# Transposing finished feed-forward blocks by DMA in 16-bit halves instead of on TensorE

## The chip, the cores and the metric

The kernel runs on one core of one Trainium2 chip. The metric is the device time of one execution, in microseconds, as the median over runs. One core has five engines with an instruction stream each: TensorE (PE in the profile; its weight loads are shown as PEld), VectorE (DVE), ScalarE (ACT), GpSimd (POOL) and SyncE (SP, which here only issues DMAs). Each takes its own instructions in order and waits on semaphores for the others.

## What is computed

A decoder trunk of two layers on 512 tokens of width 1024. Each layer is a half-step SwiGLU feed-forward block, a token mixing part (three kinds of attention, gated and merged), and a second half-step SwiGLU, with RMS norms around each. In the kernel the four feed-forward blocks are named a0, c0, a1, c1. What matters here is the SwiGLU:

```
def _swiglu(t, w_gate, w_up, w_down):
    return (jax.nn.silu(t @ w_gate) * (t @ w_up)) @ w_down
...
    for l in range(DEPTH):
        f = _swiglu(_rmsnorm(h, ffn1_pre_g[l]), ffn1_w_gate[l], ffn1_w_up[l], ffn1_w_down[l])
        h = h + 0.5 * _rmsnorm(f, ffn1_post_g[l])
...
        f = _swiglu(_rmsnorm(h, ffn2_pre_g[l]), ffn2_w_gate[l], ffn2_w_up[l], ffn2_w_down[l])
        h = h + 0.5 * _rmsnorm(f, ffn2_post_g[l])
```

The hidden width is 2816, 22 tiles of 128 columns. All data is float32; each factor of a product is split into a high and a low part, and three matmuls stand for one product.

## The kernel before

**A feed-forward block** (`ffn`). Sixteen of the 22 hidden tiles are computed in two column groups (`ci` 0 and 1) of 1024 columns. In each group the gate and then the up projection is one 2x2 block matrix product (tokens in two halves, output columns in two halves) done by seven block products instead of eight (`token_product`, products 0 to 6 in the order 0, 2, 1, 3, 4, 5, 6). So the main stretch of a block is: gate group 0 (G0), up group 0 (U0), gate group 1 (G1), up group 1 (U1), then the down projection's fourteen block products (`product`), with six remaining hidden tiles computed plainly in between. A product runs over four tiles `kk` of the contraction, and for each over two output banks `e`, with three matmuls of 128x512 each (lines 204 to 206 of the profile): 24 matmuls. `PLAN` writes the order out by hand; a queue object feeds it, loads weights ahead, and a scheduler then fixes each engine's order.

**Weights** arrive by DMA from SyncE's queue (lines 248 and 296) into raw tiles, are combined where a product needs a difference (line 326, VectorE; tiles `tg`, `tu`, `bt`), cast to the high part by ScalarE (line 181, `wh`) and subtracted by VectorE to the low part (line 182, `wl`). `wh` and `wl` have four buffers each, which are two products' worth.

**What a product leaves.** Its sums lie in two PSUM banks, with tokens on the partitions. Products 2 and 3 are copied out by ScalarE (line 775), products 4 and 5 are added by VectorE (line 777), and in an up group the products 1 and 6 are multiplied from PSUM with the gate's block (line 779), those of 4 and 5 after the addition (line 784). So after the products 1, 4, 5 and 6 of an up group one block of the hidden activations is finished, 128 partitions x 1024 (four hidden tiles' quarter for two token tiles), in the gate's tile (`sa`, `sc`). Products 3, 5 and 6 add on in the banks that product 0 opened.

**The transposes.** The down projection needs the hidden activations with hidden columns on the partitions (`hr`, from which `first_factor` makes its operands). So every finished block is transposed. `turn` does it in the next product, after that product's third tile `kk`: eight TensorE transposes of 128x128 (line 800), four into each of two PSUM banks, and a copy of each bank into `hr` by ScalarE (line 802). Over the kernel that is 4 feed-forward blocks x 2 up groups x 4 blocks = 32 times.

Of the kernel before, what the change touches and what calls it, by code (L numbers as in the profile page):

```python
# [9 lines left out]
F32 = mybir.dt.float32  # L10
F32R = mybir.dt.float32r
BF16 = mybir.dt.bfloat16
AF = mybir.ActivationFunctionType
ALU = mybir.AluOpType
AX = mybir.AxisListType
# [2 lines left out]
P = 128  # L18
# [4 lines left out]
def kernel(  # L23
# [38 lines left out]
    nc = tc.nc  # L62
    _, S, D = x.shape
# [3 lines left out]
    ND = D // P  # L67
# [21 lines left out]
    make_identity(nc, ident)  # L89
    ident16 = cst.tile([P, P], BF16, name="ident16")  # L90
    eps_t = cst.tile([P, 1], F32, name="eps_t")
    nc.vector.memset(eps_t[:], D * EPS)
    one_t = cst.tile([P, 1], F32, name="one_t")
    nc.vector.memset(one_t[:], 1.0)
    causal16 = cst.tile([P, P], BF16, name="causal16")
    sel = cst.tile([104, NH], F32, name="sel")

    def tmp(name):
        return sb.tile([P, S], F32, tag="f32t", bufs=5, name=name)
# [3 lines left out]
    def stile(shape, tag, name, dt=F32R):  # L103
        return sb.tile(shape, dt, tag=tag, bufs=BUFS[tag], name=name)
# [4 lines left out]
    def pbank(tag, name):  # L109
        return ps.tile([P, S], F32, tag=tag, bufs=4, name=name)  # L110
# [67 lines left out]
    def split(h_ap, l_ap, src, scale=None, later=False):  # L178
# [4 lines left out]
        else:  # L183
            both = [nc.scalar.activation(h_ap, src, AF.Copy, scale=scale)]  # L184
            make = lambda: nc.vector.scalar_tensor_tensor(l_ap, src, scale, h_ap.bitcast(F32), ALU.mult, ALU.subtract)  # L185
# [7 lines left out]
    def sigmoid_neg(t, z, c):  # L193

        b, minus = nbgate[:, c[0], c[1]:c[1] + 1], bgate[:, c[0], c[1]:c[1] + 1]
        nc.scalar.activation(t, z, AF.Abs, bias=b)
        nc.scalar.activation(t, t, AF.Exp, scale=-1.0)
        nc.scalar.activation(t, t, AF.Ln, bias=one_t[:])  # L198
        nc.vector.scalar_tensor_tensor(t, z, minus, t, ALU.max, ALU.add)  # L199
        nc.scalar.activation(t, t, AF.Exp, scale=-1.0, bias=minus)  # L200

    def mm3(pt, lh, ll, rh, rl, start, stop, free=False):

        nc.tensor.matmul(pt, lh, rh, start=start, stop=False, skip_group_check=free)  # L204
        nc.tensor.matmul(pt, lh, rl, start=False, stop=False, skip_group_check=free)  # L205
        nc.tensor.matmul(pt, ll, rh, start=False, stop=stop, skip_group_check=free)  # L206
# [271 lines left out]
    def rstd(st, a, b=None):  # L478

        s, m, y, w = st[:, a:a + 1], st[:, 3:4], st[:, 4:5], st[:, 5:6]  # L480
        if b is None:
            nc.scalar.activation(y, s, AF.Ln, bias=eps_t[:])
            nc.vector.tensor_scalar(m, s, D * EPS, None, ALU.add)
# [113 lines left out]
    ORDER = (0, 2, 1, 3, 4, 5, 6)  # L597
    SUM = (0, 1, 2, 0, 2, 0, 0)
    TO = ((0, 0), (0, 0), (1, 1), (0, 1), (0, 1), (1, 1), (1, 0))
    park = [nc.dram_tensor(f"park{i}", (NT, P, D), F32, kind="Internal").ap() for i in range(2 * L)]  # L600

    def ffn(l, src, wg, wu, wd, dst, name, spare, parked, plan, aside=None):
# [4 lines left out]


        hid, st = {}, {}
        hr = {}  # L610
        f0 = NC * FC
        tags = ["q"] * 2 + ["o"] * 4
        act = lambda k, c=FULL: quad_act(src.us)(k, c)
# [1 line left out]
        def hidden_rows(i):  # L615
            if i not in hr:
                hr[i] = stile([P, FC // 2, S], ("k", "tri")[i // 2], f"hr{name}_{i}", F32)
            return hr[i]
# [114 lines left out]
        def in_product(n):  # L733
            if n in (0, 1, 6):
                i, j = ((0, 0), (0, 1), None, None, None, None, (1, 1))[n]
                return [block(i, j, part) for part in range(2)]
            return st["u", n]

        def token_product(ci, up, n, uns):

            nm = f"{name}{'gu'[up]}_{ci}_{n}"
            if n in (0, 1, 2):
                st["c", n] = [pbank("z" if n == 0 else "mm", f"pw{nm}_{e}") for e in range(2)]
            if n == 1:
                for e in range(2):
                    nc.scalar.copy(st["c", 1][e][:], st["c", 0][e][:])
            if n == 0:
                if not up:
                    st["s", ci] = {}
            pts = st["c", SUM[n]]  # L750
            h, l = in_product(n)
            opens, ends = n in (0, 2), n in (1, 4, 6)
            for un in uns:
                for k in range(un.nk):
                    kk = un.k0 + k
                    for e in range(2):
                        c = slice(e * P, (e + 1) * P)
                        mm3(pts[e][:], h[:, kk, c], l[:, kk, c], un.h[:, k], un.l[:, k], opens and kk == 0,
                            ends and kk == ND // 2 - 1, free=True)
                        yield 3 * S * PE_US  # L760
                    if kk == ND // 2 - 2:
                        yield from turn("z")
            if n == 0:
                return
            q = TO[n]
            g = st["s", ci]
            if not up and q not in g:
                g[q] = stile([P, FC // 2, S // 2], "f", f"s{name}_{ci}_{q[0]}{q[1]}", F32)[:]
            g = g[q]
            r = hidden_rows(2 * ci + q[1])[:, :, HALVES[q[0]]] if up else g  # L770
            for e in range(2):
                p = pts[e][:].rearrange("p (f q) -> p f q", f=2)
                re, ge = r[:, 2 * e:2 * e + 2], g[:, 2 * e:2 * e + 2]
                if n in (2, 3):
                    nc.scalar.copy(re, p)
                elif n in (4, 5):
                    nc.vector.tensor_tensor(re, re, p, ALU.add)
                elif up:
                    nc.vector.tensor_tensor(ge, p, ge, ALU.mult)
                else:  # L780
                    nc.scalar.activation(re, p, AF.Silu)
            if n in (4, 5):
                if up:
                    nc.vector.tensor_tensor(g, r, g, ALU.mult)
                else:
                    nc.scalar.activation(r, r, AF.Silu)
            if up and n in (1, 4, 5, 6):
                st["turn"] = (f"{nm}", g, r)

        def turn(tag):  # L790

            nm, g, r = st.pop("turn", (None, None, None))
            if nm is None:
                return
            g = g.rearrange("p f q -> p (f q)")
            for b in range(2):
                pt = pbank(tag, f"ht{nm}_{b}")
                for f in range(2):
                    for e in range(2):
                        nc.tensor.transpose(pt[:, (2 * f + e) * P:(2 * f + e + 1) * P],  # L800
                                            g[:, e * S + (2 * b + f) * P:][:, :P], ident[:])
                nc.scalar.copy(r[:, 2 * b:2 * b + 2], pt[:].rearrange("p (f q) -> p f q", f=2))
                yield 0.4
# [42 lines left out]
        def product(at, uns):  # L846
            ci, n = DOWN[at]
            first, last = ci == 0, ci == NC - 1
            if at == 0:
                RINGS["o"] = 2  # L850
                dst.begin()
            if at + 1 < len(DOWN):
                first_factor(*DOWN[at + 1])
            if first and n in (0, 2):
                st["b", SUM[n]] = [pbank("z", f"pd{name}_{n}_{e}") for e in range(2)]
            pts = st["b", SUM[n]]
            h, l = st.pop(("a", ci, n))
            opens, ends = first and n in (0, 2), last and n in (1, 4, 6)
            for un in uns:
                for k in range(un.nk):  # L860
                    kk = un.k0 + k
                    for e in range(2):
                        c = slice(e * P, (e + 1) * P)
                        mm3(pts[e][:], h[:, kk, c], l[:, kk, c], un.h[:, k], un.l[:, k], opens and kk == 0,
                            ends and kk == FC // 2 - 1, free=True)
                        yield 3 * S * PE_US
                    if kk == FC // 2 - 2:
                        yield from turn("mm")
            if not last:
                return  # L870
            if n == 0:
                st["b", 1] = [pbank("z", f"pd{name}_1_{e}") for e in range(2)]
                for e in range(2):
                    nc.scalar.copy(st["b", 1][e][:], pts[e][:])
                return
            i, hf = TO[n]
            for e in range(2):
                f = dst.fs[2 * i + e][:, HF[hf]]
                if n in (4, 5):
                    nc.vector.tensor_tensor(f, f, pts[e][:], ALU.add)  # L880
                else:
                    nc.scalar.copy(f, pts[e][:])
# [767 lines left out]

    wps, wsb = pbank("z", "warm"), tmp("warm").bitcast(BF16)
    nc.vector.memset(wsb[:, 0:S], 0.0)
    mc = None
    for l in LAYERS:
        i, mn = 3 * l, []
# [44 lines left out]
```

## Time and profile before

| | |
|---|---|
| median of 3 runs | 2388.64 us (2386.66 to 2390.05) |
| profiled execution, its own time | 2394.11 us |
| its span in the profile | 2392.4 us |
| mean granted TensorE clock | 0.998 |
| TensorE busy | 2371.8 us, 99% of the span |
| VectorE busy | 1807.0 us, 76% |
| ScalarE busy | 1416.7 us, 59% |
| DMA, mean over the span | 141 GB/s |

Busy times are merged spans, so matmuls that overlap count once. A row of a group gives line, engine, operation, the tiles written and read with buffer numbers left out, the count, the merged busy time and the mean of one instruction in ns, and the idle time of the engine before it with what ended it. A row of the timeline gives the start, the length, engine, line and operation; several equal ones may be merged (x8). In the waits and the chain, "PE pwc0u L206" names engine, tile and line. `pwc0u` is the PSUM tile of the up products of the block c in layer 0.

### The profile page before, as it was taken

The page shows a single profiled execution, that of the slowest core. Times are in us where ns is not written, and L with a number is a line of the kernel's source. Part 1 is how long each engine was busy: PE and PEld are TensorE (multiplying, and loading weights), DVE is VectorE, ACT ScalarE, POOL GpSimd, SP SyncE. Part 2 cuts the span into 40 slices and gives each one's busy share as a digit, 9 for nine tenths or more (in the row PEclk, how much of TensorE's full clock was granted, in tenths as well). Part 3 has the DMA queues.
Part 4 walks back from the last instruction along what each step waited for, and adds up shares of the span by engine and source line. Part 5 has one row for each costly group of instructions (what it writes and reads, how often), then busy time and mean ns, then how long its engine had stood idle before and what let it go on. Part 6 is the DMA issues. An engine that isn't in the chain of part 4 may idle for free.

```text
span 2392.4 us, 31521 instructions
## 1 busy us (share of the span) xinstructions
PE 2371.8 (99%) x11975; PEld 2007.0 (84%) x11975; DVE 1807.0 (76%) x2358; ACT 1416.7 (59%) x2242; POOL 75.1 (3%) x134
## 2 busy tenths in 40 slices
PE   9999999999999999999999999999999999999998
PEld 7788889888888888888888888889888888888887
DVE  8876877676777689778788778766767767887685
ACT  6655565576766555554655545656777664655544
POOL 1000000000111000000000000000001100000000
PEclk9999999999999999999999999999999999999999
DMA  6654455223323655544645544542323235555443
GB/s 203 185 149 142 159 189 146 80 82 87 89 72 106 197 173 176 146 144 152 222 139 166 167 150 144 200 123 71 94 75 97 80 115 194 164 180 159 150 150 141
DMA packets 232172, 338.22 MB, mean 141 GB/s; under 512 B 10683, under 2 KB 125395, under 8 KB 232021
## 3 DMA queue, kind: packets, MB, share of 16 engines
q1 hardware_dynamic: 231924, 336.18, 44.9%
q8 instruction: 94, 1.54, 0.3%
q14 instruction: 58, 0.47, 0.1%
q0 software_dynamic: 96, 0.03, 0.0%
HBM read 319.39 MB, written 16.78 MB: 141 GB/s over the span
## 4 chain that ended last, share of the span: by engine, by line
PE 90%; DVE 4%; DMA 2%; ACT 2%; issue 1%; SPq 0%; POOL 0%; DVEq 0%; ACTq 0%
PE pg L204 3%; PE pg L206 3%; PE pg L205 3%; PE pdc L205 3%; PE pdc L206 3%; PE pda L205 3%; PE pdc L204 3%; PE pda L204 3%; PE pda L206 3%; PE pb L206 2%; PE pb L204 2%; PE pb L205 2%; PE pq L204 1%; PE pq L205 1%; PE pk L205 1%
## 5 line engine op out<-in xcount | busy, mean ns | idle before, releaser
L204 PE MATMUL pg<-us_a,wh_wg 128*128 128x512 f32 x384 | 151.2, 394 | 0.0
L206 PE MATMUL pg<-us_a,wl_wg 128*128 128x512 f32 x384 | 149.9, 390 | 0.0
L205 PE MATMUL pg<-us_a,wh_wg 128*128 128x512 f32 x384 | 149.8, 390 | 0.0
L205 PE MATMUL pda<-wl_da,aha 128*128 128x512 f32 x224 | 87.9, 392 | 0.2 <-DVE wl_da L182 0.2
L205 PE MATMUL pdc<-wl_dc,ahc 128*128 128x512 f32 x224 | 87.7, 392 | 0.0
L181 ACT CAST wh_da<-raw_da 128x1024 fp32r<-128x1024 f32 x50 | 52.2, 1051 | 59.9 <-PE pda L206 18.7
L206 PE MATMUL pda<-wh_da,ala 128*128 128x512 f32 x224 | 87.4, 390 | 0.0
L206 PE MATMUL pdc<-wh_dc,alc 128*128 128x512 f32 x224 | 87.3, 390 | 0.0
L204 PE MATMUL pda<-wh_da,aha 128*128 128x512 f32 x224 | 86.8, 390 | 0.0
L204 PE MATMUL pdc<-wh_dc,ahc 128*128 128x512 f32 x224 | 86.8, 390 | 0.0
L206 PEld LDWEIGHTS pg<-us_a,wl_wg 128*128 128x128 f32 x384 | 72.1, 188 | 15.3
L182 DVE TENSOR_TENSOR wl_da<-raw_da,wh_da 128x1024 fp32r<-128x1024 f32 x50 | 60.8, 1223 | 31.4 <-ACT wh_da L181 31.0
L204 PEld LDWEIGHTS pg<-us_a,wh_wg 128*128 128x128 f32 x384 | 72.2, 188 | 14.0
L205 PEld LDWEIGHTS pg<-us_a,wh_wg 128*128 128x128 f32 x384 | 72.2, 188 | 14.0
L182 DVE TENSOR_TENSOR wl_dc<-raw_dc,wh_dc 128x1024 fp32r<-128x1024 f32 x50 | 61.0, 1223 | 30.2 <-ACT wh_dc L181 29.8
L181 ACT CAST wh_dc<-raw_dc 128x1024 fp32r<-128x1024 f32 x50 | 52.4, 1051 | 51.6 <-PE pdc L206 19.0
L185 DVE SCALAR_TENSOR_TENSOR wl_wg<-raw_wg,wh_wg 128x1024 fp32r<-128x1024 f32 x48 | 58.4, 1221 | 21.6 <-ACT wh_wg L184 21.6
L199 DVE SCALAR_TENSOR_TENSOR ga<-pg,bgate,ga 128x512 f32<-128x512 f32 x48 | 35.9, 747 | 49.6 <-ACT ga L198 49.6
L181 ACT CAST wh_uc<-raw_uc 128x1024 fp32r<-128x1024 f32 x44 | 46.3, 1052 | 43.8 <-PE pwc1u L206 10.3
L181 ACT CAST wh_ua<-raw_ua 128x1024 fp32r<-128x1024 f32 x44 | 46.1, 1051 | 32.6 <-PE pwa1u L206 10.3
L184 ACT ACTIVATE wh_wg<-raw_wg 128x1024 fp32r<-128x1024 f32 x48 | 50.5, 1057 | 24.1 <-PE pv L1092 11.7
L182 DVE TENSOR_TENSOR wl_uc<-raw_uc,wh_uc 128x1024 fp32r<-128x1024 f32 x44 | 53.7, 1220 | 12.1 <-ACT wh_uc L181 12.1
(651 smaller groups left out, 8006.3 us busy)
## 6 DMA issues: line engine op xcount, KB each, us to landing
raw_da<-in_ffn_w_down_dram SPq DMA_DIRECT2D x66, 512.0 KB, 4.4
raw_dc<-in_ffn_w_down_dram SPq DMA_DIRECT2D x66, 512.0 KB, 3.9
raw_ga<-in_ffn_w_gate_dram SPq DMA_DIRECT2D x52, 512.0 KB, 3.8
raw_ua<-in_ffn_w_up_dram SPq DMA_DIRECT2D x52, 512.0 KB, 4.1
raw_gc<-in_ffn_w_gate_dram SPq DMA_DIRECT2D x52, 512.0 KB, 3.8
raw_uc<-in_ffn_w_up_dram SPq DMA_DIRECT2D x52, 512.0 KB, 3.8
raw_wg<-in_w_gate_dram SPq DMA_DIRECT2D x48, 512.0 KB, 3.5
raw_wo<-in_w_out_dram SPq DMA_DIRECT2D x24, 512.0 KB, 3.6
```

The lines of the kernel that those rows point to most:

```text
L181: both = [nc.scalar.copy(h_ap, src)]
L182: make = lambda: nc.vector.tensor_tensor(l_ap, src, h_ap.bitcast(F32), ALU.subtract)
L184: both = [nc.scalar.activation(h_ap, src, AF.Copy, scale=scale)]
L185: make = lambda: nc.vector.scalar_tensor_tensor(l_ap, src, scale, h_ap.bitcast(F32), ALU.mult, ALU.subtract)
L199: nc.vector.scalar_tensor_tensor(t, z, minus, t, ALU.max, ALU.add)
L204: nc.tensor.matmul(pt, lh, rh, start=start, stop=False, skip_group_check=free)
L205: nc.tensor.matmul(pt, lh, rl, start=False, stop=False, skip_group_check=free)
L206: nc.tensor.matmul(pt, ll, rh, start=False, stop=stop, skip_group_check=free)
```

## The change

The blocks of products 1, 4 and 6 of every up group are transposed by DMA, the block of product 5 by TensorE as before. In the second tile `kk` of the product behind, ScalarE splits the float32 words of the block into two tiles of 16-bit words (low and high halves, `th`). In the third tile, SyncE issues for each of them one transposing DMA, SBUF to SBUF, 128x1024 16-bit words (`tr`). Three products further on, ScalarE puts the transposed words back into `hr`, every second 16-bit word, the low half in the first tile and the high half in the third. The products of the down projection call the same step, so the last blocks of a group finish there. The tiles for it come from the five temporary buffers (`tmp`) and, for products 1 and 6, from the buffer tagged "rs". The scheduler may set each of these instructions earlier or later on its engine; in the changed program's order the put-backs stand earlier than the source has them, a few instructions behind the splits.

```
+    DMA_TURNS, OWN_PLANES = {1: 0, 4: 0, 6: 0}, (1, 6)
...
-        hr = {}
+        hr, turns = {}, []
...
                         yield 3 * S * PE_US
+                    dma_turn(kk)
                     if kk == ND // 2 - 2:
                         yield from turn("z")
...
-            if up and n in (1, 4, 5, 6):
+            if up and n in DMA_TURNS:
+                turns.append([nm, g, (2 * ci + q[1], q[0]), n in OWN_PLANES, -DMA_TURNS[n], None, None])
+            elif up and n in (1, 4, 5, 6):
                 st["turn"] = (f"{nm}", g, r)
+
+        def dma_turn(kk):
+
+            for one in turns:
+                nm, g, (row, i), own, age, parts, planes = one
+                if kk == 1 and age == 0:
+                    one[5] = parts = [tmp(f"th{nm}_{h}")[:].bitcast(U16) for h in range(2)]
+                    words = g.rearrange("p f q -> p (f q)").bitcast(U16)
+                    for h in range(2):
+                        nc.scalar.copy(parts[h], words[:, h::2])
+                if kk == 2 and age == 0:
+                    one[6] = planes = ([stile([P, 2, 2 * S], "rs", "tr" + nm, U16)[:, h] for h in range(2)] if own else
+                                       [tmp(f"tr{nm}_{h}")[:].bitcast(U16) for h in range(2)])
+                    for h in range(2):
+                        nc.sync.dma_start_transpose(planes[h].rearrange("p (r q) -> p r q", q=P), parts[h])
+                if kk in (0, 2) and age == 3:
+                    r, h = hidden_rows(row)[:].bitcast(U16), kk // 2
+                    nc.scalar.copy(r[:, :, i * S + h:(i + 1) * S:2].rearrange("p f (e q) -> p e f q", e=2),
+                                   planes[h].rearrange("p (e f q) -> p e f q", e=2, q=P))
+                if kk == ND // 2 - 1:
+                    one[4] += 1
+            turns[:] = [one for one in turns if one[4] < 4]
...
                         yield 3 * S * PE_US
+                    dma_turn(kk)
                     if kk == FC // 2 - 2:
                         yield from turn("mm")
```

More of the change, by code (lines that the diff above doesn't have):

```diff
@@ L12 @@
 BF16 = mybir.dt.bfloat16
+U16 = mybir.dt.uint16
 AF = mybir.ActivationFunctionType
```

## The prediction

> **What bounds the kernel now.** The page comes first, for the busy shares and for the chain that ended last.
>
> ```profile
> span 2392.4 us, 31521 instructions
> PE 2371.8 (99%) x11975; PEld 2007.0 (84%) x11975; DVE 1807.0 (76%) x2358; ACT 1416.7 (59%) x2242; POOL 75.1 (3%) x134
> PE 90%; DVE 4%; DMA 2%; ACT 2%; issue 1%; SPq 0%; POOL 0%; DVEq 0%; ACTq 0%
> ```
>
> TensorE is busy 99% of the span and carries 90% of the chain, so time taken from TensorE's stream comes off the end unless another engine then holds TensorE up. The profiled execution took 2394.11 us around its span of 2392.4; the median of the runs is 2388.64, which is 5.47 less. I work out a difference against the profiled execution and take the same difference from the median. A measurement of this kernel can tell about 0.2%, or 4.8 us, from no change.
>
> Next I read what an up group's stretch looks like, since the whole change lies there and in the products just behind. The windows are the two up groups of one layer's second feed-forward block (DVE is VectorE, ACT is ScalarE).
>
> ```profile
> core 0: us, PE busy (x) PEld busy (x) DVE busy (x) ACT busy (x) POOL busy (x), PEclk, DMA share, GB/s
> 922.00:961.00 39.00, 38.80 (x180) 32.03 (x179) 32.22 (x30) 21.08 (x26) 0.00 (x0) 1.00 0.59 175
> 1002.60:1041.50 38.90, 38.71 (x180) 31.86 (x179) 32.42 (x32) 23.64 (x29) 0.00 (x0) 1.00 0.46 136
> ```
>
> TensorE is full here too, VectorE has some 6.6 us free in 39, ScalarE 15 to 18, and the DMA engines are about half busy, at the full granted clock (1.00).
>
> **Part 1, what is removed: TensorE's transposes.** All rows of the line that transposes finished blocks, by feed-forward block, and one row of its copy out of PSUM:
>
> ```profile
> L800 PE MATMUL hta0u<-ident,sa x64: 270/273/303, 98.4 to 205.1; 128*128 128x128 f32 x64
> L800 PE MATMUL htc0u<-ident,sc x64: 271/273/273, 942.5 to 1048.6; 128*128 128x128 f32 x64
> L800 PE MATMUL hta1u<-ident,sa x64: 270/273/273, 1285.0 to 1392.3; 128*128 128x128 f32 x64
> L800 PE MATMUL htc1u<-ident,sc x64: 270/273/273, 2130.1 to 2236.1; 128*128 128x128 f32 x64
> L802 ACT COPY hrc<-htc0u x16: 586/590/595, 943.1 to 1048.9; 128x512 f32<-128x512 f32 x16
> ```
>
> Four times 64 transposes are 32 blocks of eight. The change leaves eight blocks (product 5 in each of the eight up groups) and moves 24. The 273 ns of one instruction is not its price, because matmuls overlap. The price is the extra distance between the matmuls on either side, read from the timeline of TensorE around the first block of the second feed-forward block:
>
> ```profile
> 942.05 0.39 PE L205 MATMUL pwc0u<-wl_uc,uhc 128*128 128x512 f32 x1
> 942.28 0.39 PE L206 MATMUL pwc0u<-wh_uc,ulc 128*128 128x512 f32 x1
> 942.51 1.03 PE L800 MATMUL htc0u<-ident,sc 128*128 128x128 f32 x8
> 943.30 0.48 PE L204 MATMUL pwc0u<-wh_uc,uhc 128*128 128x512 f32 x1
> 943.62 0.40 PE L205 MATMUL pwc0u<-wl_uc,uhc 128*128 128x512 f32 x1
> ```
>
> Matmuls start 0.23 us apart. Across the block the distance is 943.30 - 942.28 = 1.02, which is 0.79 too much, and the next step is 0.32, another 0.09 to 0.10: 0.89 us a block. So 24 x 0.89 = **21.3 us** leave TensorE's stream. The upper end is the merged busy time, 1.03 us a block, which gives 24.7.
>
> **Part 2, what ScalarE gets.** Each moved block loses two copies of 0.59 us and gains four of 128x1024: two that pick the low and the high 16-bit words apart, two that put the transposed words back. A copy of that many elements is in the trace as a cast:
>
> ```profile
> L181 ACT CAST wh_uc<-raw_uc 128x1024 fp32r<-128x1024 f32 x44 | 46.3, 1052 | 43.8 <-PE pwc1u L206 10.3
> ```
>
> At 1.05 us, 24 x (4 x 1.05 - 2 x 0.59) = 72 us more on ScalarE, 1417 to about 1489 of some 2370. Up to three blocks fall into one up group, 9 us on 21 to 24 of 39: it fits, and throughput is not the danger. No row shows a 16-bit copy with a stride; at one and a half times 1.05 us it would be 14 to 15 us a group more than now, still inside 39. VectorE gets nothing new.
>
> **Part 3, order and deadlines.** ScalarE takes its instructions in order, so a put-back that waits for its DMA holds everything behind it. In the changed program's order the first block (product 1) runs on ScalarE like this: weight cast, split low, split high, weight cast, put back low (waits for its transposing DMA), weight cast, the two copies that empty product 3's PSUM banks, weight cast, put back high (waits likewise), weight cast. Before, the same stretch is:
>
> ```profile
> 938.63 1.05 ACT L181 CAST wh_uc<-raw_uc 128x1024 fp32r<-128x1024 f32 x1 [1.62 <-PE pwc0u L206]
> 941.35 1.05 ACT L181 CAST wh_uc<-raw_uc 128x1024 fp32r<-128x1024 f32 x1 [1.67 <-PE pwc0u L206]
> 944.28 0.59 ACT L775 COPY hrc<-pwc0u 128x512 f32<-128x512 f32 x1
> 944.96 1.06 ACT L181 CAST wh_uc<-raw_uc 128x1024 fp32r<-128x1024 f32 x1
> 945.92 0.58 ACT L775 COPY hrc<-pwc0u 128x512 f32<-128x512 f32 x1
> 950.40 1.05 ACT L181 CAST wh_uc<-tuc 128x1024 fp32r<-128x1024 f32 x1 [1.66 <-PE pwc0u L206]
> 938.18 1.28 DVE L779 TENSOR_TENSOR sc<-pwc0u,sc 128x512 f32<-128x512 f32 x2
> 947.04 1.22 DVE L182 TENSOR_TENSOR wl_uc<-raw_uc,wh_uc 128x1024 fp32r<-128x1024 f32 x1
> 952.37 1.22 DVE L182 TENSOR_TENSOR wl_uc<-tuc,wh_uc 128x1024 fp32r<-128x1024 f32 x1
> 950.20 0.39 PE L204 MATMUL pwc0u<-wh_uc,uhc 128*128 128x512 f32 x1
> 952.92 0.39 PE L204 MATMUL pwc0u<-wh_uc,uhc 128*128 128x512 f32 x1
> 959.72 0.39 PE L204 MATMUL pwc0u<-wh_uc,us_b 128*128 128x512 f32 x1
> 954.21 1.23 DVE L182 TENSOR_TENSOR wl_gc<-raw_gc,wh_gc 128x1024 fp32r<-128x1024 f32 x1 [0.62 <-ACT wh_gc L181]
> 963.33 0.39 PE L204 MATMUL pwc0g<-wh_gc,us_b 128*128 128x512 f32 x1
> ```
>
> The finished block is there at 938.18 + 1.28 = 939.46. ScalarE ends its cast at 939.68, the low split at 940.73, the high split at 941.78, the next cast at 942.83. Let L be the time from the end of a split to its transposed half in place, SyncE's issue included. Then the low half goes back at 940.73 + L to 941.78 + L, the cast behind ends at 942.83 + L, and product 3's two copies at 944.00 + L. TensorE opens product 5, which adds into those banks, at 950.20, and now 0.89 earlier: 949.31. So **L may be 5.3 us** before TensorE waits. The weight in that stretch has more room: its cast ended at 946.02, its subtraction at 948.26, its use is at 952.92 (952.03 now), so it may be 3.8 late, which allows L up to 7.0.
>
> The high half's DMA stands on SyncE's queue behind two weight loads, the second of which waits until about 945.85 for its slot:
>
> ```profile
> 938.29 3.05 SPq L296 DMA_DIRECT2D tgc<-in_ffn_w_gate_dram  x2
> 945.85 9.98 SPq L296 DMA_DIRECT2D raw_gc<-in_ffn_w_gate_dram  x5
> raw_gc<-in_ffn_w_gate_dram SPq DMA_DIRECT2D x52, 512.0 KB, 3.8
> gsave<-ga SPq DMA_DIRECT2D x16, 256.0 KB, 2.1
> raw_q<-in_w_in_dram SPq DMA_DIRECT2D x16, 512.0 KB, 3.9
> gb<-gsave SPq DMA_DIRECT2D x16, 256.0 KB, 4.1
> hfa<-park SPq DMA_DIRECT2D x4, 512.0 KB, 6.4
> ```
>
> It is issued at about 946.3 and lands at 950.3 if L is 4.0, at 954.1 if the 3.8 us load ahead must pass first. Then the put-back and the cast behind it end at 952.4 to 956.2, against 951.45 before. That weight's subtraction ended at 953.59 and its use is at 959.72, so 6.1 less 0.9 is spare and at most 4.8 is used. Hidden, if narrowly at the upper end. The blocks of products 4 and 6 share ScalarE with casts for the group behind, which run some 8 us ahead of their use (the first subtraction ends at 955.44, the weight is used at 963.33), and in a second up group with the first casts for the down products; I count them as hidden where the first block is.
>
> **L, the unknown.** No transposing DMA is in this trace. A half is 256 KB in 128 rows of 2 KB. Four rows above are near: a plain 256 KB out of SBUF lands after 2.1 us, 256 KB into SBUF after 4.1, 512 KB in 512-byte pieces after 3.9, and the slowest group of loads after 6.4. From 2.1 to 6.4, I take 4.0, by raw_q, whose load (1,024 pieces) has as many pieces as a half cut into 128-word rows. At 4.0 the deadline of 5.3 holds; at 6.4 it is missed by 1.1 us in each of eight groups, 9 us. I charge 3.5 us for that, somewhat under halfway between 0 and 9. Among the pages, the Trainium skill, "Advanced Engine Details and Errata", section X-Bar Transpose (TRN2), says that such DMAs go as fast as ordinary ones; that would keep L near the plain rows and the loss at nil, and no run here shows it yet.
>
> SyncE: 48 DMAs more, and each split's DMA now stands ahead of weight loads. The load of the second tgc at about 941 waits for the low split (940.73) and then for the transpose's issue. The weights behind are wanted a group later, so a microsecond or two here costs nothing; a second tgc late by that much holds VectorE, whose weight subtraction behind it (947.04) has 3.8 us to spare.
>
> **The sum.** -21.3 + 3.5 = **-17.8 us**, 2394.1 to 2376.3 for the profiled execution, 2388.6 to 2370.8 for the median. Ends of the terms: -24.7 with nothing lost (2363.9), -21.3 + 9 (2376).
>
> **The rivals.** *The put-back waits (slower).* If each half lands late, ScalarE is held in order at every put-back. The place is product 3's PSUM copies ahead of product 5, and it decides from L = 5.3 on. Say a half takes the slowest row, 6.4, and passes one 3.8 us load first: L = 10.2, 4.9 over, in eight groups 39 us, and -21.3 + 39 = +18. Held again as long at the block of product 4, where the casts are 8 us ahead and VectorE would run into the delay, it is 78, or +57. In the middle is 2426. For it: half the DMA time is taken already (0.59 share), and the trace has no transpose to go by. Against it: the loads of this very stretch, raw_gc, land in 3.8 us, and so do the plain rows of a half's size, in 2.1 and 4.1. The Trainium skill, "VectorE: DVE Perf Modes", section The three transpose paths, gives 1,309 ns for one 128x128 square through the DMA crossbar; if the eight squares of a half went one behind the other at that price, my estimate is 10.5 us for a half, which is this rival. Its advice to keep a transpose on TensorE speaks against the change as well. I give it 24 in 100.
>
> *The loss is not small but partial.* L between 5.3 and 8, one to two and a half microseconds late in the eight groups, 8 to 20 us of the 21 given back: -13 to -1, around 2381. For it: the margin of 5.3 is only a third over my 4.0. Some 16 in 100; the later half of it is the case of no change, to which I also count a strided copy that costs twice and uses ScalarE's slack up.
>
> *The transposes were hidden anyway.* Then nothing is gained. Against it: the matmul after the block starts 0.79 us late in the rows above, and TensorE has no idle time to fill. 3 in 100. That the change does not do what it says is excluded by the program's order: 48 transposing DMAs, and 192 transposes fewer on TensorE.
>
> **How the numbers follow.** The forecast has 57 in 100. With the better part of the partial loss, 9 in 100: faster by over 0.2% 0.66, within 0.2% 0.09 (the hidden case and the worst of the partial one), slower 0.25 (the late put-back and a tail). The likeliest time is 2371, and its case alone would span 2364 to 2376. The range runs from 2364, the merged busy time with nothing lost, up to 2415, which takes in the partial loss and the lower half of the late put-back (2407 to 2446); under 2 in 10 is left out, most of it above.
>
> **What would show it.** Right: merged busy time of L800's successor down to a quarter, some 2347 us of TensorE; product 3 to product 5 of an up group 0.9 us shorter without a wait; four 1.05 us copies a block on ScalarE, 1489 us in all; transposing DMAs landing in about 4 us. Wrong: ScalarE idle before its put-backs for several microseconds, TensorE waiting for "L775"'s copies or for wl weights in the up groups, landings over 5.3 us, or copies of 16-bit words well over 1.05 us.

## The result and the profile after

The changed kernel takes 2394.36 us (median of 10 runs, 2392.17 to 2396.51) where the kernel before takes 2388.31 on the same chip (10 runs, 2386.19 to 2390.05): ratio 1.0024, 95% interval 1.0016 to 1.0033, 6 us slower. The forecast was 17.8 us faster.

The page of the changed kernel (first the span, then each engine's busy time, then the chain that ended last):

```profile
span 2390.8 us, 31245 instructions
...
PE 2355.4 (99%) x11783; PEld 1989.9 (83%) x11783; DVE 1805.7 (76%) x2358; ACT 1489.9 (62%) x2290; POOL 73.7 (3%) x134
...
PE 88%; DVE 4%; ACT 3%; DMA 3%; issue 2%; SPq 0%; POOL 0%; DVEq 0%; ACTq 0%
```

192 transposes are gone and ScalarE's busy time rose by 73 us, as forecast. TensorE's merged busy time fell by 16.4 us. The sign that the forecast named, 24.7 less (2347 us), was too much to ask, because 1.03 us a block counts the overlap with the neighbouring matmuls; the rest of the gap is matmuls that became slower (below). What came back are waits of TensorE. The list of waits of the changed kernel (tile and line that waited, what released it; us in total, times, longest):

```profile
PE pwa0u L205 <- ACT wh_ga L182: 3.4, 1, 3.4
PE pwc0u L205 <- ACT ahc L182: 2.8, 1, 2.8
PE pwa0u L205 <- ACT aha L182: 2.3, 1, 2.3
PE pwa1u L205 <- ACT aha L182: 2.2, 1, 2.2
PE pwc1u L205 <- ACT ahc L182: 1.8, 1, 1.8
PE pwc0u L205 <- ACT wh_gc L182: 1.7, 1, 1.7
PE pwc1u L205 <- ACT wh_gc L182: 1.7, 1, 1.7
PE pwa1u L205 <- ACT wh_ga L182: 1.4, 1, 1.4
```

All eight stand at the same point, the first matmul of product 6 in each of the eight up groups: 17.3 us. Before, the wait at that point is 0.2 us a group. The releaser named is a cast that ended late; what TensorE waits for there is VectorE, as the timeline shows.

The timeline around one of them, product 1's block to the opening of the next gate group in the second feed-forward block; ScalarE first, then VectorE, then the two matmuls on either side of the wait:

```profile
941.07 1.99 ACT L803 COPY thc0u<-sc 128x1024 uint16<-128x1024 uint16 x2
...
946.11 1.36 ACT L811 COPY hrc<-trc0u 128x1024 uint16<-128x1024 uint16 x1 [2.10 <-DMA trc0u<-thc0u]
...
951.96 1.36 ACT L811 COPY hrc<-trc0u 128x1024 uint16<-128x1024 uint16 x1 [1.67 <-DMA trc0u<-thc0u]
953.17 1.05 ACT L182 CAST wh_uc<-tuc 128x1024 fp32r<-128x1024 f32 x1
954.12 1.06 ACT L803 COPY thc0u<-sc 128x1024 uint16<-128x1024 uint16 x1
955.06 1.07 ACT L182 CAST wh_gc<-raw_gc 128x1024 fp32r<-128x1024 f32 x1
...
960.49 2.57 ACT L811 COPY hrc<-trc0u 128x1024 uint16<-128x1024 uint16 x2 [2.47 <-DMA trc0u<-thc0u]
...
954.26 1.23 DVE L183 TENSOR_TENSOR wl_uc<-tuc,wh_uc 128x1024 fp32r<-128x1024 f32 x1 [0.26 <-ACT wh_uc L182]
956.16 1.23 DVE L183 TENSOR_TENSOR wl_gc<-raw_gc,wh_gc 128x1024 fp32r<-128x1024 f32 x1 [0.67 <-ACT wh_gc L182]
957.30 1.28 DVE L780 TENSOR_TENSOR hrc<-hrc,pwc0u 128x512 f32<-128x512 f32 x2
...
956.01 0.39 PE L207 MATMUL pwc0u<-wh_uc,ulc 128*128 128x512 f32 x1
958.13 0.47 PE L205 MATMUL pwc0u<-wh_uc,us_b 128*128 128x512 f32 x1 [1.73 <-ACT wh_gc L182]
```

Read it backwards. Product 6 may open when VectorE has added product 5's sums (L780). That addition stands on VectorE behind the low part of a weight for the next group (wl_gc, 956.16), which waits for its cast on ScalarE (955.06). The weight is not wanted before the next group, but VectorE is in order. ScalarE is late because two put-backs and a split stand ahead of that cast, and the put-backs wait for their DMAs.

ScalarE in that stretch, by windows of the changed kernel (busy time of each engine in the order that the first line names; ACT, the fourth, is ScalarE):

```profile
core 0: us, PE busy (x) PEld busy (x) DVE busy (x) ACT busy (x) POOL busy (x), PEclk, DMA share, GB/s
941.00:964.50 23.50, 21.77 (x100) 17.67 (x100) 16.03 (x16) 17.26 (x20) 0.00 (x0) 1.00 0.85 229
114.60:120.60 6.00, 5.99 (x15) 4.70 (x16) 2.73 (x3) 2.98 (x3) 0.00 (x0) 0.52 1.10 286
```

17.26 us of work and 2.10 + 1.67 + 2.47 = 6.24 us of waiting for transposing DMAs make 23.50 of 23.50: ScalarE has nothing left there. The third of these waits, 2.47 us, comes after product 6 has opened, so it cannot have delayed that opening; up to the late cast ScalarE did nothing but work and wait for the first two. The second row is another effect. After the 3.4 us wait in the first block TensorE ran at a granted clock of 0.52 for 6 us, and 13 matmuls came 0.43 us apart in place of 0.23; the first of them:

```profile
114.61 0.77 PE L205 MATMUL pwa0u<-wh_ua,us_x 128*128 128x512 f32 x1 [3.37 <-ACT wh_ga L182]
115.18 0.63 PE L206 MATMUL pwa0u<-wl_ua,us_x 128*128 128x512 f32 x1
115.60 0.63 PE L207 MATMUL pwa0u<-wh_ua,us_x 128*128 128x512 f32 x1
```

The Trainium skill, "TensorE: Matmul & The Clock Gate", Part 1, says that TensorE's clock falls to half after an idle window of about 3.4 us and comes back after a busy one. The trace agrees on the halves, with 0.52. The length of one wait alone does not decide here, since a 1.8 us wait (at 2222 us) was followed by seven slow matmuls and a 2.85 us wait (at 1040 us) by none.

### The profile page after: what moved, and what is told of

Its sections match the earlier page's. It is cut to its first block, busy times and chain, and to the rows that moved or that the text cites. A ratio compares the mean times of both kernels' runs of the same rounds, so it can differ in the third digit from the quotient of the medians.

```text
span 2390.8 us, 31245 instructions
## 1 busy us (share of the span) xinstructions
PE 2355.4 (99%) x11783; PEld 1989.9 (83%) x11783; DVE 1805.7 (76%) x2358; ACT 1489.9 (62%) x2290; POOL 73.7 (3%) x134
## 4 chain that ended last, share of the span: by engine, by line
PE 88%; DVE 4%; ACT 3%; DMA 3%; issue 2%; SPq 0%; POOL 0%; DVEq 0%; ACTq 0%
PE pg L206 4%; PE pg L207 4%; PE pg L205 4%; PE pda L206 3%; PE pda L207 3%; PE pda L205 3%; PE pdc L206 2%; PE pdc L207 2%; PE pdc L205 2%; PE pb L207 2%; PE pb L206 2%; PE pb L205 2%; PE pq L205 1%; PE pq L206 1%; PE pwo L206 1%
## 5 line engine op out<-in xcount | busy, mean ns | idle before, releaser
L182 ACT CAST wh_da<-raw_da 128x1024 fp32r<-128x1024 f32 x50 | 52.1, 1050 | 51.8 <-DMA raw_da<-in_ffn_w_down_dram 17.3
L183 DVE TENSOR_TENSOR wl_uc<-raw_uc,wh_uc 128x1024 fp32r<-128x1024 f32 x44 | 53.7, 1220 | 16.6 <-ACT wh_uc L182 16.4
L185 ACT ACTIVATE wh_wg<-raw_wg 128x1024 fp32r<-128x1024 f32 x48 | 50.5, 1057 | 24.1 <-PE pv L1120 11.7
L183 DVE TENSOR_TENSOR wl_ua<-raw_ua,wh_ua 128x1024 fp32r<-128x1024 f32 x44 | 53.6, 1220 | 14.0 <-ACT wh_ua L182 13.9
```

What stands on the lines that cost most here:

```text
L182: both = [nc.scalar.copy(h_ap, src)]
L183: make = lambda: nc.vector.tensor_tensor(l_ap, src, h_ap.bitcast(F32), ALU.subtract)
```

## The experiments

Each ratio is to runs of the kernel before on the same chip, taken alongside. Line numbers differ a little between kernels.

**The kernel before again.** No edit.

> The kernel before, unchanged, for a profile from the same chip and call as the next three. The first profile of it lies 5 us above the median of its runs. If that is noise of that one execution, this profile comes out at a span of 2386 to 2389, the waits at product 6 stay at 0.2 us each, and the waits outside the up groups are some 4 us shorter; if the profile is always slower than the timed runs, it is 2392 again.

Measured: 2391.18 against 2390.55 (ratio 1.0002, 0.9992 to 1.0012). Rows of its page, its waits and its windows:

```profile
span 2385.6 us, 31521 instructions
...
PE pwc0u L204 <- DVE hrc L777: 0.4, 2, 0.2
...
936.50:960.00 23.50, 23.31 (x114) 19.18 (x113) 17.58 (x19) 11.65 (x14) 0.00 (x0) 1.00 0.64 182
```

The last row is ScalarE's stretch as above: 11.65 us busy of 23.5, before the change.

The first profile came from an execution 5.5 us over its median, so I compare the changed kernel with this one: spans 2385.6 and 2390.8, 5.2 more, near the 6 of the medians. From the starts of all matmuls in the feed-forward blocks, counting what exceeds the usual 0.227 us between two: about 21 us of transposes are gone, the waits rose from about 4 to about 25, and matmuls at half rate and small steps add about 6. That sums to some 5 or 6.

**No transposes at all.** In the place of splits, DMAs and put-backs:

```
+            if kk == 2 and "plain" in st:
+                g, r = st.pop("plain")
+                for b in range(2):
+                    nc.scalar.copy(r[:, 2 * b:2 * b + 2], g[:, 2 * b:2 * b + 2])
```

> This kernel leaves the transposition of the three moved blocks out altogether: in the place of the splits, the transposing DMAs and the put-backs stand two plain 128x512 copies on ScalarE, about 0.6 us each, as before the change, with no DMA and no TensorE work. It is the ceiling of what taking 24 blocks off TensorE can give. If the removed transposes are worth the 0.89 us a block that I counted, the time is 21 us under the kernel before, 2367; if the copies are not in anyone's way, no wait at the opening of product 6 is over 0.5 us. If the rival holds that TensorE's transposes were worth much less in the stream (16 us of busy time, or nothing), it is 2372 to 2388.

Measured: 2375.85 against 2390.43, ratio 0.9942 (0.9930 to 0.9954): 14.6 us, not 21. TensorE waited 0.8 us at product 6 in seven groups and 3.3 us in the first, over the 0.5 us of the first branch.

**VectorE's order.** In the changed kernel, the low parts of the two weight units loaded during product 5 of an up group are issued behind product 5's addition:

```
+            if Q.put_off is not None:
+                Q.put_off.append((self.split_from(src, later=True), self))
+                return
...
+            if up and n == 5:
+                Q.lows()
```

> The changed kernel, and on VectorE alone the weight subtractions that belong to product 5's stretch of an up group (one of them waits for a late cast on ScalarE) stand behind the addition of product 5's sums instead of ahead of it. My theory: TensorE waits at the opening of product 6 because that addition is queued behind a subtraction that waits for ScalarE. Then the extra 1.6 to 3.5 us at product 6 in each of the eight up groups go, some 18 us, and what follows them (a stretch at half rate, 4.6 us in the two places seen) with them: 2370 to 2376. If the wait at product 6 came from ScalarE's copies or DMAs directly, or if the subtraction put later makes its own weight late for the next group's first products, nothing is gained: 2390 to 2396.

Measured: 2388.30, ratio 0.9990 (0.9981 to 0.9999), between the two branches: some 8 us better than the changed kernel, 2 better than before. The waits at product 6 shrank to 6.3 us in all and others grew, at the opening of the next gate group, where TensorE needs the banks that ScalarE copies out (L842) behind a put-back:

```profile
PE pwc1g L205 <- ACT hrc L842: 2.9, 1, 2.9
PE pwa0u L205 <- DVE hra L791: 2.8, 2, 1.6
PE pwa0g L205 <- ACT hra L842: 2.7, 1, 2.7
```

So the order on VectorE is a way by which ScalarE's lateness reaches TensorE, and not the only one.

**Both together:** plain copies as in the first, VectorE's order as in the second.

> The first experiment (three blocks copied by ScalarE and not transposed, no DMA) with the second's order on VectorE: the addition of product 5's sums ahead of the weight subtraction that waits for ScalarE. The first experiment gave 14.6 us of the 21.3 that left TensorE's stream, and TensorE waited 10 us at product 6. If that order on VectorE is all that is in the way, the waits go and it is 2367 to 2371. If the subtraction put later makes a weight late elsewhere, it stays at 2375 to 2377.

Measured: 2368.87 against 2389.99, ratio 0.9909 (0.9894 to 0.9924): 21.1 us. The 24 blocks are worth what the forecast said, and without VectorE's order a third of that is lost even with no work added on ScalarE (1419.2 us busy, 1417.0 before). The waits at product 6 in the two up groups of c0, first of the plain copies, then with the order:

```profile
PE pwc0u L205 <- DVE hrc L780: 1.6, 2, 0.8
```

```profile
PE pwc0u L205 <- DVE hrc L791: 0.4, 2, 0.2
```

**Put-backs on GpSimd** (`nc.gpsimd.tensor_copy` for `nc.scalar.copy`).

> The changed kernel, with the put-backs on GpSimd in place of ScalarE, so ScalarE never waits for a transposing DMA (48 us of its idle time now) and loses 48 copies of 1.36 us. My theory, with ScalarE's lateness as the root: its casts are back in time, VectorE's chain no longer waits, and the waits at product 6 go: 2368 to 2376. If ScalarE's splits, not its put-backs, make the casts late, the waits at product 6 stay at 1 us and more: about 2385. If GpSimd's copies hold up VectorE (by a common way to the memory) the subtractions and additions on VectorE become longer and it is 2390 or more.

Measured: 2406.19, ratio 1.0068 (1.0054 to 1.0082), the third branch. VectorE's busy time rose by 25 us, to 1830.6. In the timeline:

```profile
952.76 1.34 POOL L811 COPY hrc<-trc0u 128x1024 uint16<-128x1024 uint16 x1 [190.75 <-DMA trc0u<-thc0u]
954.09 1.23 DVE L327 TENSOR_TENSOR tgc<-tgc,raw_gc 128x1024 f32<-128x1024 f32 x1 [1.61 <-issue]
968.64 2.03 DVE L183 TENSOR_TENSOR wl_gc<-tgc,wh_gc 128x1024 fp32r<-128x1024 f32 x1 [1.46 <-ACT wh_gc L182]
```

VectorE started its next instruction when GpSimd's copy ended (954.10), waiting for nothing that the profile shows, and a subtraction of 1.22 us beside another such copy took 2.03. The put-backs on GpSimd hold up VectorE, so this run does not say what a free ScalarE would give. The Trainium skill, "GPSIMD Engine Reference", section 1. Specifications, states that GpSimd shares VectorE's ways to SBUF and that instructions with two SBUF inputs contend; the subtraction has two, and the trace agrees.

**Put-backs at their place in the source**, three products behind (`tc.keep_in_program_order` around L811's copy).

> The changed kernel, with each put-back at the place on ScalarE at which the source has it, three products later, instead of where the scheduler drew it ahead: the DMAs have landed long before. This takes the DMA wait away and leaves ScalarE's work as it is (the put-backs still take 1.36 us each). If the wait for the DMA is what makes the casts late, the waits at product 6 go and it is 2370 to 2378. If it is the added work on ScalarE (the two splits of the block of product 4 stand right ahead of the late cast in either order), the waits at product 6 stay near 2 us: 2385 to 2394.

Measured: 2394.68, ratio 1.0020 (1.0011 to 1.0028), as slow as the changed kernel. The waits for DMAs on ScalarE fell from 47.7 to 18.3 us and those at product 6 from 17.3 to 10.8, but 6.2 us came up in the down products. (The 12 and 7.5 us that the next expectations name are the same waits, counted from start to start of the matmuls.) Less DMA wait gained nothing there.

**Splits at their place in the source** (the same around L803's copies).

> The changed kernel, with the splits kept at their place in the source: on ScalarE the two splits of product 4's block stand behind the two weight casts for the next group instead of ahead of and between them. If the split ahead of the cast is the root, the wait at product 6 falls from 1.6 to 3.5 us to 0.9 or less in each of the eight groups, 11 to 15 us; the put-back of that block is then later by 2 us and may hold the two copies out of PSUM at the next group's opening, which costs up to 2 us in four places: 2378 to 2388. If the DMA wait of product 1's put-back is the root, the wait at product 6 stays over 1.5 us and it is 2390 to 2396.

Measured: 2395.82, ratio 1.0024 (1.0015 to 1.0033). The waits at product 6 stayed at 1.2 to 4.6 us. The split ahead of the cast is not the root by itself. The run is not a clean test of it: the edit also moved product 1's splits, from 0.1 us to 5.3 us behind the finished block, so that this block's put-backs came later too.

**Both at their place.**

> Splits and put-backs are both kept at their place in the source: no wait for a DMA on ScalarE and no split ahead of the casts. With put-backs alone kept there, TensorE waited 12 us at product 6 and 7.5 us more in the down products. If split and DMA wait act together, the waits at product 6 fall to about 0.6 us each and the down products' waits stay: minus 21 for the transposes, plus 4, plus 7, so 2379 to 2384. If the copies' mere work on ScalarE (15 of 39 us free in a group) were the limit, the waits at product 6 stay at 1.5 us and it is 2390 or more.

Measured: 2396.31, ratio 1.0025 (1.0015 to 1.0035). Neither branch: the waits at product 6 fell to 0.4 us, except one of 1.6, and yet nothing was gained; they turned up at the openings of other groups and in the down products. My theory of one bad place fell with this run.

**Both at their place, without DMAs, and with DMAs that nobody reads.** The put-backs read `parts[h]` in place of `planes[h]`, with the DMAs left out in the first and kept in the second.

> The kernel with splits and put-backs kept at their place in the source, without the transposing DMAs: the put-backs read the split halves as they are, so this leaves the transposition out. ScalarE has the same 96 extra copies in the same places; it never waits for a transposing DMA (36 us of its idle time in that kernel), and SyncE issues weight loads alone. If ScalarE's added work and order are what gives the gain back, it stays at 2390 to 2396. If the waits for the DMAs, and the DMAs' place on SyncE's queue, give it back, it comes down to the kernel with no transposition and plain copies: 2376 to 2381.

> The same, but the 48 transposing DMAs run and nobody reads what they write; the put-backs read the split halves (the transposition is left out of the result). The order of ScalarE's instructions is that of the run without DMAs. If what the DMAs cost is their place on SyncE's queue, ahead of weight loads, and their traffic, this takes 8 us or more over the run without them. If the cost is ScalarE's wait for their landing, this stays within 3 us of the run without them, and the kernel whose put-backs do wait is 10 us or more above both.

Measured: 2378.33 (0.9948, 0.9936 to 0.9961) and 2382.75 (0.9969, 0.9958 to 0.9981) against 2389.99; the kernel with read DMAs had lost 5.8 us against its own runs of the kernel before. So, from before: -11.7 with ScalarE's 96 copies alone, -7.2 with the DMAs beside them, +5.8 when the put-backs depend on them. The dependence is the largest step, 13 us, the traffic and SyncE's issues 4.4, so the second branch is the nearer one. The 13 are not only the wait for landing: SyncE's order is not the same in the two (with read DMAs the second halves of the blocks of products 1 and 6 stand several weight loads later, that of product 6 five).

**The block of product 4 left on TensorE**, and the same with VectorE's order:

```
-    DMA_TURNS, OWN_PLANES = {1: 0, 4: 0, 6: 0}, (1, 6)
+    DMA_TURNS, OWN_PLANES = {1: 0, 6: 0}, (1, 6)
```

> Only the blocks of products 1 and 6 go by DMA; those of products 4 and 5 stay on TensorE. 16 blocks at 0.89 us leave TensorE's stream, 14 us. If the two splits of the block of product 4, ahead of the cast that VectorE waits for, make the wait at product 6, that wait is back at 0.2 to 0.5 us and the time is 2375 to 2380. If the put-backs of product 1's block, held by their DMAs in the same stretch, make it, the wait stays at 1.5 us or more in each of eight groups: about 2388.

> The blocks of products 1 and 6 by DMA, those of products 4 and 5 by TensorE, and the second experiment's order on VectorE. Without that order TensorE waited 7.6 us at product 6 and the time was 7 us under the kernel before. If the order takes those waits away, it is 2377 to 2380, under both kernels; if the DMA waits on ScalarE only move on to the next group's opening, 2383 to 2386.

Measured: 2384.01 against 2390.55 (0.9970, 0.9958 to 0.9982), and with the order 2378.42 against 2389.99 (0.9950, 0.9937 to 0.9962): the first between its branches, the second as expected, 11.6 us under the kernel before, where the changed one is 6 over. It is the fastest version here that transposes everything.

**The block of product 4 alone by DMA** (`{4: 0}`), and with VectorE's order.

> Only the block of product 4 goes by DMA; those of products 1, 5 and 6 stay on TensorE. 7.1 us (8 blocks at 0.89) leave TensorE's stream. If this block costs by itself (its splits stand ahead of the cast that VectorE waits for, whatever ScalarE did before), the wait at product 6 is 1.0 to 2 us in each of eight groups and the time is 2390 to 2396 beside 2390.5 before. If it costs only because product 1's put-backs have held ScalarE before it, the wait stays under 0.6 us and it is 2383 to 2387.

> The same, with VectorE's order of the second experiment (product 5's addition ahead of the weight subtraction). If the block's cost is VectorE's order at product 6, the waits there go and the time is 2383 to 2386. If the put-backs that wait for its DMAs just before the next group's opening cost as much, TensorE waits 1.4 to 3 us at the openings that follow a first up group instead, and it is 2387 to 2392.

Measured: 2388.30 against 2390.12 (0.9990, 0.9981 to 0.9999), and 2383.84 (0.9973, 0.9962 to 0.9984). In the first the wait at product 6 is 0.7 us, in one group 2.0, between the branches. In the second it is 0.2, and one opening behind waits 1.4: the first branch.

These four with the changed kernel show that the blocks cost together what they do not cost apart. The figures are us against the kernel before:

| blocks by DMA | off TensorE | measured | with VectorE's order |
|---|---|---|---|
| 1 and 6 | -14.2 | -6.5 | -11.6 |
| 4 | -7.1 | -1.8 | -6.3 |
| sum of the two rows | -21.3 | -8.3 | -17.9 |
| 1, 4 and 6 | -21.3 | +6.0 | -2.1 |

Blocks 1 and 6 and block 4 each gain; together they lose 14 to 16 us more than their sum, with either order on VectorE. That they meet on ScalarE is read from the windows of the same 23.5 us, blocks 1 and 6 first, then block 4 alone:

```profile
938.30:961.80 23.50, 23.31 (x111) 19.19 (x110) 18.56 (x18) 15.02 (x19) 0.00 (x0) 1.00 0.75 210
```

```profile
939.00:962.50 23.50, 22.82 (x110) 18.77 (x109) 16.42 (x16) 15.06 (x18) 0.00 (x0) 1.00 0.71 202
```

ScalarE is busy for 15.0 us in both, and its timelines have 3.3 and 1.8 us of waiting for DMAs in them: 18.3 and 16.8 of 23.5. With all three blocks it is 23.5 of 23.5.

**Blocks 1 and 6 with VectorE's order and late put-backs.**

> Blocks of products 1 and 6 by DMA, of 4 and 5 by TensorE, VectorE's order of the second experiment, and the put-backs kept at their place in the source, three products behind, where fewer of them wait. The same without the late put-backs took 11.6 us off of the 14.1 that leave TensorE. If the rest is ScalarE's wait for DMAs, the time is 2375 to 2377. If the late put-backs hold the first down products instead (as in the fourth experiment, 7.5 us of waits there), it is 2380 to 2385.

Measured: 2399.90 against 2391.24, ratio 1.0038 (1.0025 to 1.0050). The place of the put-backs alone costs 20 us against the sister run; ScalarE's waits for DMAs fell from 47.5 to 19.7 us, while 9.5 us of waits came up in the down products and most others in the up groups, at their openings above all. Both branches were too good: early put-backs that wait are the better choice here.

**Everything at its place, and VectorE's order.**

> The changed kernel with splits and put-backs at their place in the source and VectorE's order of the second experiment. Without that order it took 2396.3 and TensorE waited 0.5 us at each product 6, but 28 us in all, at the openings of other groups and in the down products. If ScalarE's wait for DMAs makes those, the order changes little: 2390 to 2396. If VectorE's order was what carried the lateness on, it falls to 2376 to 2383, the run in which the DMAs are unread.

Measured: 2393.87, ratio 1.0010 (1.0001 to 1.0019), in the first branch's range: the order changes little there.

**The transposing DMAs on ScalarE's queue** (`nc.scalar.dma_start_transpose`).

> The changed kernel with the transposing DMAs issued from ScalarE's own queue, right behind the splits, and SyncE issuing weight loads alone. If an issue holds ScalarE as long as it held SyncE, 1.23 us, ScalarE gets 59 us more to do. If SyncE's queue makes the second halves late (8.9 us from split to put-back where the first took 4.0), ScalarE's wait before put-backs falls from 48 us to under 20; the time then depends on the 59 us: 2390 to 2400. If the transfer itself is what takes long, the wait stays near 48 us and the 59 us come on top: over 2400.

Measured: 2415.11, ratio 1.0101 (1.0086 to 1.0117), the third branch. An issue took 1.25 us of ScalarE's queue, the wait before the put-backs stayed at 46 us, and TensorE's waits at product 6 grew to 32 us. The landing:

```profile
DMA to landing us min/median/max: 3.1/5.6/10.1
```

Taking SyncE's queue away does not remove the wait. Whether the transfer alone would make it is not shown, since the landing became longer as well (median 5.6 us against 3.9).

## Why the prediction was wrong

**The gain, right.** 21.3 us were forecast for the 24 blocks. Plain copies with VectorE's order gave 21.1, and the starts of matmuls show about 21 gone.

**L, right, and its deadline nearly irrelevant.** The transposing DMAs of the changed kernel:

```profile
L808 SPq DMA_TRANSPOSE trc0u<-thc0u x12: 1231/1232/2029, 942.2 to 1052.9; - x12
DMA to landing us min/median/max: 3.0/3.9/5.6
```

The first half of product 1's block was split by 942.07 and put back from 946.11: 4.04 us for a forecast of 4.0. The second, behind two weight loads on SyncE (one of them waiting for its slot), went out at 947.55 and was in place at 951.96. This execution ran 1.49 us later than the one that I forecast from (product 1's block was finished at 940.95 and not at 939.46), so that is within 0.2 us of my 946.3 and 950.3. The hit is in part luck: the rows left L anywhere from 2.1 to 6.4, and no run tests the count of pieces by which I chose 4.0. Product 3's copies were in time, as the deadline of 5.3 us promised, in all groups but one, where TensorE waited 0.8 us for them. The Trainium skill, "Advanced Engine Details and Errata", section X-Bar Transpose (TRN2), says that transposing DMAs go as fast as ordinary ones. The trace agrees only in part: 3.9 us for 256 KB stands beside 4.0 us for an ordinary 256 KB into SBUF (gb), but beside 2.1 us for one out of it (gsave), and most ordinary weight loads moved 512 KB in 3.4 to 4.4 us. The 10.5 us that I worked out from "VectorE: DVE Perf Modes", section The three transpose paths, is not seen: eight squares together land in 3.9.

**The copies.** The splits took 1.04 us (1.05 forecast). The put-backs, which write every second 16-bit word, took 1.36 and not 1.05, 0.3 us on 48 of them. That the busy time still rose by the forecast 73 us is luck: the instructions' own times rose by 86 us, and instructions that follow each other at once overlap (two splits take 1.99 us and not 2.08), which merged busy time counts once.

**The step that failed: Part 3's "I count them as hidden where the first block is", and with it the 3.5 us charged for all waits.** The sum had -21.3 + 3.5. The first term came true, and in place of the second stood about 27 us of added waits and slow matmuls. For the casts behind the put-backs and splits I compared their end with the matmul that uses the weight, some 8 us later. The first to be late was another: VectorE's addition of product 5's sums, behind the subtraction that waits for that cast. The row of 954.21 showed VectorE waiting 0.62 us for such a cast before the change, ahead of that addition. The next rows of the same timeline, before the change, show how little was spare:

```profile
956.06 1.36 DVE L777 TENSOR_TENSOR hrc<-hrc,pwc0u 128x512 f32<-128x512 f32 x2 [0.62 <-PE pwc0u L206]
956.89 0.47 PE L204 MATMUL pwc0u<-wh_uc,us_b 128*128 128x512 f32 x1 [0.20 <-DVE hrc L777]
```

The addition waited 0.62 us for TensorE, so a cast could be 0.62 us late there, not 8. It is the same in seven of the eight up groups, and in the changed kernel the addition follows the subtraction without a gap in all eight. The 0.89 us of transposes inside product 5 were the cover, and they are more than 0.62. Taking the 24 blocks away, with no work added on ScalarE, gave back 6.5 of 21.1 us. In that run the plain copies of product 4's block also stand ahead of the cast, so the share of the cover alone is not separated.

**What made the casts late: Part 2's "it fits, and throughput is not the danger".** I set 9 us a group against the 15 to 18 free in 39. Its test with slower copies was also off: at one and a half times 1.05 us three blocks add 15.4 us, and 23.64 + 15.4 is no longer inside the second group's 38.9. But the copies of the first two blocks, and the put-backs of both, fall within the 23.5 us from product 1's block to the next group's opening, and ScalarE's waits for DMAs belong to its load, since it is in order. There it was busy 11.65 us before (second profile) and has 17.26 + 6.24 after. The prediction allowed for the wait and for the work, each against its own slack, never for both in one stretch. The work alone does nearly fit: in the source's order the 96 copies without DMAs gained 11.7 us where the plain copies gained 14.6. The experiments by blocks show the rest: either set of blocks gains, both together lose 14 to 16 us more.

**The rivals.** The one that came nearest was the put-back that waits, which I tied to L over 5.3 us. Its place and its threshold were wrong: the put-backs' waits hurt already at L = 4.0, together with the copies, and at product 6. The hidden transposes are excluded by the 21.1 us.

**What stays open.** How much of the 14 to 16 us is ScalarE's own work and how much its wait for DMAs was not separated in the changed kernel's own order. In the order of the source the wait and SyncE's order together made 13 us of 17.5, but that order has other waits. Nor was it separated whether the third block's DMAs, the temporary buffers that it holds or SyncE's order add to what its copies cost on ScalarE. What the half clock costs in a run without a profile is not known.

## What to carry to other kernels

Before work is moved to an engine that looks half idle, add up its load in the stretch between the two deadlines that surround the new work, with every wait for a DMA counted as load. For each instruction that becomes late, ask what stands behind it on the engines that wait for it, and not only when its own result is used. Two changes that each fit may not fit together, so move the blocks one set at a time and keep the set that gains: here blocks 1 and 6, with one changed order on VectorE.

## What the runs showed of the hardware that I had not expected

- A ScalarE copy of 128x1024 16-bit words takes 1.04 us when it reads every second word and 1.36 us when it writes every second one.
- A transposing DMA of 128x1024 16-bit words holds the issuing queue for 1.23 us (SyncE) or 1.25 us (ScalarE); a weight load of 512 KB issued by itself in the same stretch held SyncE's for 0.37 to 0.53 us.
- A wait of TensorE can cost more than its length: after 3.4 us the clock stood at 0.52 for 6 us.
- Beside a GpSimd copy of 1.34 us VectorE stood idle until it ended, with no wait that the profile shows; with 48 such copies VectorE's busy time rose by 25 us.
